# Attention of a decoder trunk: outputs half a projection tile behind scores, and pins on exponentials, masks and sums

## The chip, the cores and the metric

The kernel runs on one core of one Trainium2 chip. The metric is device time in microseconds (us) of one execution, lower is better. Five engines work side by side, each through a queue of its own: TensorE (PE in the profile: matmuls into PSUM banks, with weight loads shown apart as PEld), VectorE (DVE), ScalarE (ACT), GpSimd (POOL), and SyncE (SP), which here issues the DMAs.

## The reference

Two layers over 1024 tokens of width 1024, in float32. The first mixes tokens by retention and RWKV-7 heads; the second, which the change is about, by sliding-window attention with sinks. Each is followed by a SwiGLU feed-forward layer. What matters here:

```python
z = h @ w_qkv + b_qkv                       # 16 query heads, 4 key/value heads, head size 64
s = einsum('bnqhgd,bnkhd->bnhgqk', q, kb) * HEAD_DIM ** -0.5    # blocks of 128 queries, 256 keys
s = where(valid, s, -inf)                   # a window of 128 keys back
m = maximum(max(s), sink)
e = exp(s - m)
p = e / (sum(e) + exp(sink - m))
o = einsum('bnhgqk,bnkhd->bnqhgd', p, vb).reshape(B, T, SWA_WIDTH) @ w_o + b_o
h = h + o
h = h + (silu(n @ w_gate) * (n @ w_up)) @ w_down                # n = rms_norm(h)
```

## The kernel before

Activations lie transposed, features on the 128 partitions and tokens along the free side, in two halves of 512 tokens. A float32 product is made of three matmuls in a shorter format: each operand is split into a high part (a rounding copy on ACT) and a low part (operand minus high part, on DVE or POOL), and high x high, high x low and low x high are added up in one PSUM bank. A projection onto 128 features is 8 steps of three matmuls, 24 in all, 512 columns each; its weights are loaded by SP (L402), split in two tiles by ACT (L432) and DVE or POOL (L433), six split tiles in rotation.

The feed-forward layer is computed with a scheme of fewer products: `form0` (L1252) normalizes the first token half into eight tiles (`normed`, L1248), splits them (ACT L462, DVE L464) and stores them; `early` (L1469) makes the first of the products. A "pair" is one gate and one up projection of it, in lockstep: first halves of both (four steps each), then each bank is copied out by ACT (`u0`, L1472), because the second half adds to the same bank.

Attention (`attn`, L1692) is written as a plan of words, executed left to right. There are 16 blocks j (token half, key/value head, two windows of 128 queries):

- S: `scores`. 40 or 48 small matmuls (L1726) into banks r, c and two m; ACT copies (L1739) and DVE predicated copies (L1740) bring them to `s`; DVE takes the maximum (L1758), then the sinks' terms (L1759, L1760); ACT makes eight exponentials (L1763, "exps j" for the first) and the sink's (L1761); DVE adds the sink's to the sum (L1766, "dens j"), inverts, multiplies (L1768) and transposes 32 x 32 blocks (L1773); SP stores the result to DRAM (`pd`).
- D: `fetch`. Four DMAs bring `pd` back as `pc` with the keys on the partitions (two buffers).
- M: `sides`. A mask product `pT` on DVE (L1787) and `pc - pT` in two halves, one on DVE and one on POOL (L1792). A mask is pinned behind the sinks of block j + 2.
- O: `out`. 12 or 16 matmuls (L1805) with the values into the one bank y; the high part is copied by ACT (L1811, "his j"), the low part made by DVE (L1812, "los j").
- q, r: half a projection of queries of the first and second token half; k: half a projection of keys or values, or a transpose of values (L1678); w: one output projection `w_o` of the first half (24 matmuls, L447 to L450, then DVE L1831); f: the normalizing factor (one matmul, L479, with L480 and L481 on ACT) and `form0`; p: half of a pair.

The order on PE is written out by hand: `ATTN_ORDER` lists banks in the order in which the program first writes them, with numbers of matmuls, and `queue` (L328) chains them. On the other engines the framework's scheduler sets the order, except where `behind` (L605) pins one instruction behind another on the same engine's queue; such a pin sets the order of issue and adds no wait of its own. PSUM has three banks f, two m, one each of r, c and y.

Of the kernel before, what the change touches and what calls it, by code (L numbers as in the profile page):

```python
# [10 lines left out]
F32 = mybir.dt.float32  # L11
F32R = mybir.dt.float32r
AF = mybir.ActivationFunctionType
ALU = mybir.AluOpType
# [120 lines left out]

ATTN_PLAN = """
S0 qqq S1 qqq D0 S2 M0 D1 qqk S3 O0 M1 D2 kkk S4 O1 M2 D3 kkk S5 O2 M3 D4 krr S6 O3 M4 D5 rrr S7 O4 M5 D6 rrr
S8 O5 M6 D7 rr S9 O6 M7 D8 S10 O7 M8 D9 wwwwk S11 kwwww rr f rr S12 rr O8 M9 D10 p S13 O9 M10 D11 pp S14 O10 M11 D12 p
S15 O11 M12 D13 pp O12 M13 D14 p O13 M14 D15 p O14 M15 p O15 p
"""  # L140
ATTN_ORDER = """
# [8 lines left out]
"""  # L150


# [102 lines left out]
class Kern:  # L255
    def __init__(self, ctx, tc, A, out):
        self.ctx, self.tc, self.nc, self.A, self.out = ctx, tc, tc.nc, A, out
        nc = self.nc
        self.pp = ctx.enter_context(tc.tile_pool(name="pp", bufs=1, side="left"))
        self.dr = ctx.enter_context(tc.tile_pool(name="dr", bufs=2, space=bass.MemoryType.DRAM))  # L260
        self.n = 0
        pad = ctx.enter_context(tc.tile_pool(name="pad", bufs=1, side="right"))
        pt = pad.tile([P, 120], F32, tag="pad", name="pad")
        nc.gpsimd.memset(pt, 0.0)
        nc.scalar.activation(pt[:, :16], pt[:, :16], AF.Copy)
        self.gapt(self.pp, 32)
        self.pv = self.t(self.pp, [P, NPV], "pv")
        nc.scalar.dma_start(self.pv, A["pvec"])
        self.cst = {}
        for nm in ("ones", "eps"):  # L270
            self.cst[nm] = self.const(self.pp, nm)
        self.h, self.plan, self.seq, self.stream = [None, None], None, {}, "-"
        self.wx, self.pin, self.rest, self.at = None, None, None, {}
        self.w6, self.nw, self.owed, self.lo = False, 0, [], self.nc.gpsimd
        self.hid = [self.dram(f"hid{i}", [FT, P, HT]) for i in range(4)]
        self.hc = [self.dram(f"hc{L}", [NP, 4, P, 2, HT]) for L in range(2)]
        self.bd = self.dram("bd", [KT, P, HT])
        self.u0s = None
        self.u0d = self.dram("u0", [NP, 2, P, HT])
        self.wsp = self.dr.tile([30, 2, P, 2, HT], F32, tag="wsp", name="wsp", bufs=1)  # L280
        self.cats = [self.dram(f"cat{hf}", [KT, P, HT]) for hf in range(2)]
# [963 lines left out]
        return self.rstd(self.kt(self.h[hf]), self.t(pool, [P, HT], "rs", 1), tag)  # L1245

    def normed(self, out, hf, k, g, r):
        self.nc.vector.scalar_tensor_tensor(  # L1248
            out=out, in0=self.kt(self.h[hf])(k), scalar=self.col(g, k), in1=r, op0=ALU.mult, op1=ALU.mult
        )  # L1250

    def form0(self, g, r, n8, sp):  # L1252

        self.X = {nm: [self.hl(n8, k + o) for k in range(4)] for nm, o in (("11", 0), ("21", 4))}
        for nm, o in (("11", 0), ("21", 4)):
            for k in range(4):
                f = self.u0(sp)
                self.normed(f, 0, k + o, g, r)
                self.nc.sync.dma_start(self.bd[k + o], f)
                self.split(f, *self.X[nm][k], False)  # L1260

# [207 lines left out]
    def early(self, ps, w, u0, use):  # L1469

        self.prod(ps, w[0](), self.X["11"], True, False)
        self.nc.scalar.copy(u0, ps)  # L1472
        yield
        self.prod(ps, w[1](), self.X["21"], False, True)
        use("11", ps)
        yield
# [141 lines left out]
    def attn_open(self, ap):  # L1618
        nc = self.nc
        m = self.const(ap, "amask").rearrange("p (m o t) -> p m o t", m=2, o=1)  # L1620
        self.own = m[:, 0].rearrange("p o (x t) -> p o x t", x=2).to_broadcast([P, 2, 2, 64]).bitcast(mybir.dt.uint32)
        self.key = m[:, 1].rearrange("p o (q t) -> p q o t", q=4).to_broadcast([P, 4, 8, 32])
        self.sink = self.t(ap, [P, 16], "sink")
        nc.scalar.dma_start(self.sink, self.A["sinks"].to_broadcast([P, 16]))
        self.nsink = self.t(ap, [P, 16], "nsink")
        nc.vector.tensor_scalar(out=self.nsink, in0=self.sink, scalar1=-1.0, scalar2=None, op0=ALU.mult)
        self.b8 = self.t(ap, [P, 8], "b8")
        nc.vector.tensor_scalar(
            out=self.b8, in0=self.pv[:, PV["bqkv"] : PV["bqkv"] + 8], scalar1=0.125, scalar2=None, op0=ALU.mult
        )  # L1630
        self.pk = self.pvt = None
        self.nu0 = 0
        self.akv, self.aq, self.ch = {}, ([], []), {}

    def proj(self, nr, ti, out, **kw):
# [56 lines left out]
    def attn(self, ap, outs, fill, plan):  # L1692
# [5 lines left out]
        pairs = [(hf, g, b) for hf in range(2) for g in range(4) for b in (0, 2)]  # L1698
        n = len(pairs)
        ds, pcs, pTs, n8, sinks = {}, {}, {}, {}, {}  # L1700

        def block(hf, g, b, tags, s):

# [41 lines left out]
        def scores(j):  # L1745
            hf, g, b0 = pairs[j]
            s = self.t(ap, [P, 2, 4, P], "s", 2)
            for i in range(2):
                block(hf, g, b0 + i, ("rc", "mm")[i], s[:, i])
            s8 = s.rearrange("p b h k -> p (b h) k")  # L1750
            st = self.t(ap, [P, 3, 8], "st", 3)
            m, den, es = (st[:, i] for i in range(3))

            def heads(t):
                return t[:, 4 * g : 4 * g + 4].rearrange("p (o h) -> p o h", o=1).to_broadcast([P, 2, 4])

            m2, es2 = (t.rearrange("p (b h) -> p b h", b=2) for t in (m, es))
            V.tensor_reduce(out=m, in_=s8, axis=AX.X, op=ALU.max, negate=True)  # L1758
            V.tensor_tensor(out=m2, in0=m2, in1=heads(self.nsink), op=ALU.min)  # L1759
            sinks[j] = V.tensor_tensor(out=es2, in0=m2, in1=heads(self.sink), op=ALU.add)  # L1760
            x = S.activation(es, es, AF.Exp)  # L1761
            for h in range(8):
                y = S.activation(s8[:, h], s8[:, h], AF.Exp, bias=m[:, h : h + 1], accum_out=den[:, h : h + 1])  # L1763
                if h == 0:
                    self.behind(y, x)
            V.tensor_tensor(out=den, in0=den, in1=es, op=ALU.add)  # L1766
            V.reciprocal(out=den, in_=den)
            V.tensor_tensor(  # L1768
                out=s8, in0=s8, in1=den.rearrange("p (h o) -> p h o", o=1).to_broadcast([P, 8, P]), op=ALU.mult
            )  # L1770

            sq = self.t(ap, [P, 4, 8, 32], "sq", 1)
            V.transpose(sq.rearrange("p k h t -> p h k t"), s8.rearrange("p h (k t) -> p h k t", k=4))  # L1773
            d = ds[j] = self.dr.tile([4, 32, 4, 2 * P], F32, tag="pd", name=f"pd_{self.n}", bufs=4)
            nc.sync.dma_start(d.rearrange("q t k x -> (q t) (k x)"), sq.rearrange("p k h t -> p (k h t)"))
# [8 lines left out]
        def sides(j):  # L1784
            pc = pcs[j]
# [3 lines left out]
                self.behind(x, sinks[j + 2])  # L1789
            for i, e in enumerate((V, G)):  # L1790
                h = slice(4 * i, 4 * i + 4)
                e.tensor_tensor(out=pc[:, :, h], in0=pc[:, :, h], in1=pT[:, :, h], op=ALU.subtract)  # L1792

        def out(j):
            hf, g, b0 = pairs[j]
# [12 lines left out]
                        )  # L1808
            tk = slice(P * b0, P * b0 + 2 * P)
            hi, lo = (n8[hf][x][:, :, tk].rearrange("p i (b t) -> p b i t", b=2) for x in (g, 4 + g))  # L1810
            S.copy(hi, po)  # L1811
            V.tensor_tensor(out=lo, in0=po, in1=hi.bitcast(F32), op=ALU.subtract)  # L1812
            self.ch[hf] = [self.hl(n8[hf], k) for k in range(KT)]

        do = dict(S=scores, O=out, M=sides, D=fetch)
        for w in plan.split():
            if w[0] in do:
                do[w[0]](int(w[1:]))
            else:
                for c in w:  # L1820
                    next(fill[c], None)

    def w_o(self, hf, ch):
        nc = self.nc
# [270 lines left out]
```

## Time and profile before

| what | value |
|---|---|
| median of 3 runs | 2266.25 us (2265.46 to 2266.54) |
| the profiled execution | 2264.58 us, of which the span of its instructions is 2261.8 us |
| granted TensorE clock, mean | 0.996 |
| busy share | PE 98%, PEld 79%, DVE 74%, ACT 45%, POOL 45% |
| the chain that ended last | PE 77%, DVE 10%, ACT 4%, the rest issue, DMA, POOL and queues |
| attention stage | some 240 us, from about 1360 to 1600 us of the span |

Times in rows of the profile are us from the start of the span. A row of the timeline gives the start, the duration, the engine, the line of the kernel, the operation, output and inputs by the program's names, their shapes, and how many; in brackets stands how long the engine was idle before it and whose end released it. A matmul's row shows how long it was in the array; matmuls overlap, so that one of 512 columns is shown at 0.39 us though the next starts sooner.

### The profile page before, as it was taken

The page shows a single profiled execution, that of the slowest core. Times are in us where ns is not written, and L with a number is a line of the kernel's source. Part 1 is how long each engine was busy: PE and PEld are TensorE (multiplying, and loading weights), DVE is VectorE, ACT ScalarE, POOL GpSimd, SP SyncE. Part 2 cuts the span into 40 slices and gives each one's busy share as a digit, 9 for nine tenths or more (in the row PEclk, how much of TensorE's full clock was granted, in tenths as well). Part 3 has the DMA queues.
Part 4 walks back from the last instruction along what each step waited for, and adds up shares of the span by engine and source line. Part 5 has one row for each costly group of instructions (what it writes and reads, how often), then busy time and mean ns, then how long its engine had stood idle before and what let it go on. Part 6 is the DMA issues. An engine that isn't in the chain of part 4 may idle for free.

```text
span 2261.8 us, 36143 instructions
## 1 busy us (share of the span) xinstructions
PE 2221.5 (98%) x13296; PEld 1784.8 (79%) x13296; DVE 1683.9 (74%) x2476; ACT 1011.3 (45%) x1914; POOL 1009.9 (45%) x784
## 2 busy tenths in 40 slices
PE   8999999999999999999999999998999999999998
PEld 6777777777878888888888887776788888888886
DVE  7877965875667358888887877987457788888876
ACT  5454544424455333333433466656444333333335
POOL 3123221202341067777787610104203677777676
PEclk9999999999999999999999999999999999999999
DMA  8565654443446545665676334444546565658663
GB/s 282 188 219 203 201 158 135 141 118 117 148 181 195 205 160 209 214 210 206 242 259 246 131 113 133 162 140 155 176 150 229 176 213 211 208 202 292 225 216 117
DMA packets 181856, 423.22 MB, mean 187 GB/s; under 512 B 44464, under 2 KB 55344, under 8 KB 181680
## 3 DMA queue, kind: packets, MB, share of 16 engines
q1 hardware_dynamic: 178272, 414.37, 53.4%
q10 hardware_dynamic: 2832, 4.45, 0.5%
q8 instruction: 105, 1.72, 0.3%
q0 software_dynamic: 576, 2.10, 0.2%
q14 instruction: 71, 0.58, 0.1%
HBM read 283.87 MB, written 131.60 MB: 184 GB/s over the span
## 4 chain that ended last, share of the span: by engine, by line
PE 77%; DVE 10%; ACT 4%; issue 3%; DMA 3%; POOL 2%; SPq 1%; DVEq 0%; POOLq 0%; ACTq 0%
PE ps_f L291 11%; PE ps_m L1306 8%; PE ps_m L1309 7%; PE ps_m L1308 7%; PE ps_m L291 6%; PE ps_f L1306 5%; PE ps_f L1308 5%; PE ps_f L1309 5%; PE ps_r L1306 2%; PE ps_c L1309 2%; PE ps_c L1306 2%; PE ps_r L1309 2%; PE ps_r L1308 2%; PE ps_c L1308 2%; PE ps_f L449 2%
## 5 line engine op out<-in xcount | busy, mean ns | idle before, releaser
L291 PE MATMUL ps_f<-n,w 128*128 128x512 f32 x1440 | 358.6, 402 | 8.6 <-ACT w L432 5.7
L291 PEld LDWEIGHTS ps_f<-n,w 128*128 128x128 f32 x1440 | 266.5, 189 | 83.4 <-issue 12.6
L433 POOL TENSOR_TENSOR w<-wr,w 128x512 fp32r<-128x512 f32 x63 | 88.3, 1411 | 294.8 <-ACT w L432 293.4
L432 ACT CAST w<-wr 128x512 fp32r<-128x512 f32 x231 | 140.7, 617 | 153.8 <-PE ps_f L450 48.7
L1306 PE MATMUL ps_f<-n,w 128*128 128x512 f32 x415 | 164.6, 397 | 0.5 <-ACT q L1472 0.5
L1309 PE MATMUL ps_f<-n,w 128*128 128x512 f32 x415 | 162.5, 392 | 0.0
L433 DVE TENSOR_TENSOR w<-wr,w 128x512 fp32r<-128x512 f32 x168 | 118.2, 708 | 59.2 <-ACT w L432 58.7
L1308 PE MATMUL ps_f<-n,w 128*128 128x512 f32 x415 | 162.2, 391 | 0.0
L433 POOL TENSOR_TENSOR w<-wq,w 128x512 fp32r<-128x512 f32 x91 | 130.8, 1449 | 31.0 <-ACT w L432 31.0
L1306 PE MATMUL ps_m<-n,w 128*128 128x512 f32 x333 | 130.4, 392 | 0.0
L1308 PE MATMUL ps_m<-n,w 128*128 128x512 f32 x333 | 129.6, 389 | 0.0
L1309 PE MATMUL ps_m<-n,w 128*128 128x512 f32 x333 | 129.5, 389 | 0.0
L1316 DVE TENSOR_TENSOR nq<-ps_m,u 128x512 f32<-128x512 f32 x88 | 58.9, 684 | 93.9 <-PE ps_m L1309 93.8
L464 POOL TENSOR_TENSOR n<-nq,n 128x512 fp32r<-128x512 f32 x60 | 100.1, 1679 | 7.6 <-ACT n L462 7.6
L1501 POOL TENSOR_TENSOR w<-wd,w 128x512 fp32r<-128x512 f32 (+1 forms) x62 | 87.1, 1414 | 33.1 <-ACT w L1500 32.7
L1306 PEld LDWEIGHTS ps_f<-n,w 128*128 128x128 f32 x415 | 77.9, 188 | 21.9 <-issue 3.8
L1306 PE MATMUL ps_m<-cb,w 128*128 128x512 f32 x236 | 91.9, 389 | 0.3 <-DVE nq L1316 0.3
L1308 PE MATMUL ps_m<-cb,w 128*128 128x512 f32 x236 | 91.8, 389 | 0.0
L1309 PE MATMUL ps_m<-cb,w 128*128 128x512 f32 x236 | 91.8, 389 | 0.0
L1309 PEld LDWEIGHTS ps_f<-n,w 128*128 128x128 f32 x415 | 77.9, 188 | 17.1 <-issue 0.7
L1501 POOL TENSOR_TENSOR w<-ws,w 128x512 fp32r<-128x512 f32 (+1 forms) x48 | 71.6, 1497 | 44.4 <-ACT w L1500 40.7
L1308 PEld LDWEIGHTS ps_f<-n,w 128*128 128x128 f32 x415 | 77.9, 188 | 16.6 <-issue 1.0
(539 smaller groups left out, 6347.9 us busy)
## 6 DMA issues: line engine op xcount, KB each, us to landing
hc<-n SPq DMA_DIRECT2D x84, 512.0 KB, 3.2
wsp<-w SPq DMA_DIRECT2D x54, 512.0 KB, 3.3
w<-wsp SPq DMA_DIRECT2D x54, 512.0 KB, 3.4
n<-hc SPq DMA_DIRECT2D x54, 512.0 KB, 6.2
wq<-in_w_gate SPq DMA_DIRECT2D x44, 512.0 KB, 4.5
u<-u SPq DMA_DIRECT2D x76, 256.0 KB, 3.1
ha<-hc SPq DMA_DIRECT2D x34, 512.0 KB, 5.2
hid<-n SPq DMA_DIRECT2D x66, 256.0 KB, 2.0
```

Source lines behind the costliest of these rows:

```text
L291: i = self.nc.tensor.matmul(out, lhsT, rhs, **kw)
L432: nc.scalar.copy(hi[:, :n], raw[:, c])
L433: self.lo.tensor_tensor(out=lo[:, :n], in0=raw[:, c], in1=hi.bitcast(F32)[:, :n], op=ALU.subtract)
L449: y = nc.tensor.matmul(ps, hi, rl, start=False, stop=False)
L464: e.tensor_tensor(out=lo, in0=src, in1=hi.bitcast(F32), op=ALU.subtract)
L1306: i = mm(ps, hi, xh, start=first and k == 0, stop=False, skip_group_check=True)
L1308: mm(ps, hi, xl, start=False, stop=False, skip_group_check=True)
L1309: mm(ps, lo, xh, start=False, stop=last and k == len(w) - 1, skip_group_check=True)
L1316: self.last_add = V.tensor_tensor(out=o, in0=x, in1=y, op=ALU.add)
L1501: nc.gpsimd.tensor_tensor(out=lo, in0=v, in1=hi.bitcast(F32), op=ALU.subtract)
```

## The change

The plan and the order of PE are rewritten, and instructions are pinned behind others.

- In the plan, output O7, two of the eight `w_o` projections and one query projection of the second half move ahead of scores S10; the other `w_o` projections and the last key/value steps are spread around S10 and S11, and one query projection less stands between `form0` and S12.
- In the order of PE, an output in most blocks follows its scores with 12 matmuls of a projection between, where before it followed at once. Pair 0's second gate half comes ahead of O9.
- New pins: the first exponential of a block behind the high copy of the first output named after its scores; the sink's sum behind the DVE half of the first mask named after its scores; masks 1 to 12 behind the low part of the output before; exponentials 12, 14 and 15 behind the first, fourth and fifth copy `u0` of the pairs; the sixth `normed` tile of `form0` behind the low part of output 8.

No instruction is added or removed. The old order of PE from S8 to S12 is `65:8 66:24 (S9) 71:6 77:18 78:18 79:18 76:8 (S10) 77:6 78:6 79:6 80:12 81:4 80:12 (S11) 87:12 86:4 87:12 88:24 89:24 90:24 91:18 92:1 91:6 93:24 (S12)`, where 71 and 76 are O6 and O7, 77 to 90 (but for 81 and 86) are `w_o` and key/value steps, 91 and 93 queries, 92 the factor. The new one is `66:12 65:8 66:12 (S9) 73:18 71:6 74:18 72:8 75:24 (S10) 73:6 74:6 80:24 81:4 82:24 (S11) 87:24 88:4 89:24 90:24 91:24 92:14 93:1 92:10 (S12)`, where 71 and 72 are O6 and O7, 73, 74, 80, 82, 87 and 89 to 91 `w_o`, 81 and 88 transposes of values, 75 and 92 queries, 93 the factor.

```diff
 ATTN_PLAN = """
 ...
-S8 O5 M6 D7 rr S9 O6 M7 D8 S10 O7 M8 D9 wwwwk S11 kwwww rr f rr S12 rr O8 M9 D10 p S13 O9 M10 D11 pp S14 O10 M11 D12 p
+S8 O5 M6 D7 rr S9 O6 M7 D8 O7 wwrr S10 M8 D9 wkw S11 wkwww rr f S12 rr O8 M9 D10 p S13 O9 M10 D11 pp S14 O10 M11 D12 p
 S15 O11 M12 D13 pp O12 M13 D14 p O13 M14 D15 p O14 M15 p O15 p
@@ form0
-                self.normed(f, 0, k + o, g, r)
+                self.formed.append(self.normed(f, 0, k + o, g, r))
@@ early
-        self.nc.scalar.copy(u0, ps)
+        self.u0copies.append(self.nc.scalar.copy(u0, ps))
@@ attn: scores, sides and out note their instructions in exps, dens, subs, his and los; then, after the plan has run:
+        at = -1
+        for w in plan.split():
+            j = int(w[1:]) if w[0] in do else -1
+            if w[0] == "S":
+                at, seen = j, set()
+            elif j >= 0 and at >= 0 and w[0] not in seen:
+                seen.add(w[0])
+                if w[0] == "O":
+                    self.behind(exps[at], his[j])
+                if w[0] == "M":
+                    self.behind(dens[at], subs[j][1])
+            if w[0] == "M" and j and j < 13:
+                self.behind(subs[j][0], los[j - 1])
+        for j, i in ((12, 0), (14, 3), (15, 4)):
+            self.behind(exps[j], self.u0copies[i])
+        self.behind(self.formed[5], los[8])
```

More of the change, by code (lines that the diff above doesn't have):

```diff
@@ L278, in __init__ @@
         self.u0s = None
+        self.u0copies, self.formed = [], []
         self.u0d = self.dram("u0", [NP, 2, P, HT])
@@ L1247, in normed @@
     def normed(self, out, hf, k, g, r):
-        self.nc.vector.scalar_tensor_tensor(
+        return self.nc.vector.scalar_tensor_tensor(
             out=out, in0=self.kt(self.h[hf])(k), scalar=self.col(g, k), in1=r, op0=ALU.mult, op1=ALU.mult
@@ L1632, in attn_open @@
         self.nu0 = 0
+        self.u0copies, self.formed = [], []
         self.akv, self.aq, self.ch = {}, ([], []), {}
@@ L1700, in attn @@
         ds, pcs, pTs, n8, sinks = {}, {}, {}, {}, {}
+        exps, dens, his, los, subs = {}, {}, {}, {}, {}
         def block(hf, g, b, tags, s):
@@ L1765, in scores @@
                     self.behind(y, x)
-            V.tensor_tensor(out=den, in0=den, in1=es, op=ALU.add)
+                    exps[j] = y
+            dens[j] = V.tensor_tensor(out=den, in0=den, in1=es, op=ALU.add)
             V.reciprocal(out=den, in_=den)
@@ L1791, in sides @@
                 h = slice(4 * i, 4 * i + 4)
-                e.tensor_tensor(out=pc[:, :, h], in0=pc[:, :, h], in1=pT[:, :, h], op=ALU.subtract)
+                y = e.tensor_tensor(out=pc[:, :, h], in0=pc[:, :, h], in1=pT[:, :, h], op=ALU.subtract)
+                if not i:
+                    subs[j] = x, y
         def out(j):
@@ L1810, in out @@
             hi, lo = (n8[hf][x][:, :, tk].rearrange("p i (b t) -> p b i t", b=2) for x in (g, 4 + g))
-            S.copy(hi, po)
-            V.tensor_tensor(out=lo, in0=po, in1=hi.bitcast(F32), op=ALU.subtract)
+            his[j] = S.copy(hi, po)
+            los[j] = V.tensor_tensor(out=lo, in0=po, in1=hi.bitcast(F32), op=ALU.subtract)
             self.ch[hf] = [self.hl(n8[hf], k) for k in range(KT)]
```

14 rows, old and new, of the table ATTN_ORDER are left out of this document.

## The prediction

> **What bounds the kernel now.** I read the table of stretches first, over the attention stage and what follows. A row gives a stretch, its length, each engine's busy time with its instructions, and after POOL the granted TensorE clock. Ahead of it stands the page's line of 40 slices for PE, in tenths.
>
> ```profile
> PE   8999999999999999999999999998999999999998
> ...
> core 0: us, PE busy (x) PEld busy (x) DVE busy (x) ACT busy (x) POOL busy (x), PEclk, DMA share, GB/s
> 1400.00:1460.00 60.00, 59.35 (x481) 45.29 (x480) 56.91 (x97) 36.89 (x133) 8.17 (x7) 1.00 0.53 176
> 1460.00:1540.00 80.00, 76.64 (x519) 60.24 (x518) 68.07 (x107) 48.69 (x136) 12.41 (x9) 1.00 0.45 153
> 1540.00:1560.00 20.00, 16.78 (x115) 12.52 (x115) 14.27 (x23) 10.63 (x42) 8.45 (x5) 0.91 0.48 153
> 1560.00:1580.00 20.00, 15.39 (x108) 11.69 (x107) 12.37 (x20) 14.36 (x40) 8.24 (x6) 0.86 0.41 127
> 1580.00:1600.00 20.00, 19.45 (x138) 14.18 (x138) 12.95 (x19) 12.66 (x33) 10.79 (x7) 0.97 0.51 170
> 1640.00:1670.00 30.00, 30.00 (x133) 24.60 (x132) 12.91 (x18) 10.00 (x16) 5.17 (x4) 1.00 0.29 101
> ```
>
> PE has work nearly always, so time can only be won where it idles or is granted a slow clock. In 1640–1670 it does not idle, one 512-column matmul starts every 30.00/133 = 0.226 us, and the slices behind stay at nine: what attention wins should reach the end of the kernel. Idle is 0.65 us in 1400–1460, 3.36 in 1460–1540, and 3.22, 4.61 and 0.55 in the last three stretches before 1600. There the clock also costs (0.09 + 0.14 + 0.03) x 20 = 5.2 us. The half-rate time behind the last two means is 2 x 0.17 x 20 = 6.8 us, ending at 1580 + 1.2, so it began at 1574.4, about 1.3 us before PE resumed (below); half of that cost nothing, and 4.55 remains. Next, the waits of the instructions in question.
>
> ```profile
> 1545.66 0.19 ACT L1761 ACTIVATE st<-st 128x8 f32<-128x8 f32 x1
> 1547.68 0.56 ACT L1811 CAST n<-ps_y 128x512 fp32r<-128x512 f32 x1
> 1549.34 0.64 DVE L1812 TENSOR_TENSOR n<-ps_y,n 128x512 fp32r<-128x512 f32 x1
> 1545.24 0.37 PE L1726 MATMUL ps_c<-ks,q 64*64 64x192 f32 x1
> 1550.03 0.65 PE L1805 MATMUL ps_y<-pT,vt 128*64 128x256 f32 x4 [3.22 <-DVE n L1812]
> 1551.19 2.28 DVE L1768 TENSOR_TENSOR s<-s,st 128x1024 f32<-128x1024 f32 x1
> 1570.61 1.28 ACT L1763 ACT_TABLE_LOAD   x1 [4.16 <-DVE st L1759]
> 1575.10 0.56 ACT L1472 COPY q<-ps_f 128x512 f32<-128x512 f32 x1
> 1575.71 0.79 PE L1306 MATMUL ps_f<-n,wx 128*128 128x512 f32 x1 [4.61 <-ACT q L1472]
> 1590.90 0.50 PE L1306 MATMUL ps_f<-n,w 128*128 128x512 f32 x1 [0.55 <-ACT q L1472]
> ```
>
> O9 waits 3.22 us for the low part of O8, the reader of the one ps_y bank; that waits for O8's high copy, which ACT runs at 1547.68, behind S12's exponentials. At 1575.71 the second half of a gate-or-up projection waits 4.61 us for the copy of its first half out of the bank (L1472); ACT had been idle 4.16 us before S14's exponentials and then put the copy behind them.
>
> Last, the chain that ended last, before S9: for every block it runs through DVE and ACT, and through no PE instruction.
>
> ```profile
> 1460.66 1.23 DVE st L1758
> 1462.18 1.21 ACT s L1763 x6
> ...
> 1468.47 1.15 DVE sq L1773
> 1470.19 1.36 DVE s L1740 x4
> ```
>
> **The change part by part.** Instructions and bytes stay the same; only places move. All numbers are of the profiled execution.
>
> *Pins of exponentials.* His8 comes ahead of exps12, and the copies u0[0], u0[3], u0[4] ahead of exps12, exps14, exps15. O9's 3.22 and the 4.61 go: O8 ends at 1539.49 (below), so ACT can run the high copy 8 us sooner; and the copy at 1575.10 fits into ACT's idle 4.16. Late next: exps12 now waits until PE has finished pair 0's first gate half, 12 matmuls (2.7 us) after O8, plus 0.6 for the copy, about 1542.8. Before, they were running at 1545.66, so this costs nothing unless DVE's maximum comes 3 us sooner; behind it on ACT stand S13's evacuations, whose PE work comes 12 matmuls later still. The other "O" pins hold already (in S13, for example, ACT's high copy precedes the exponentials) and cost nothing. With the two waits their half clock goes: 3.22 + 4.61 + 4.55 = **12.4 us won**. The 0.55 I leave in: it is u0[4] or its neighbour u0[5], and only the first is pinned (bounds 0 to 0.55).
>
> *Masks behind low parts, sink's sum behind masks.*
>
> ```profile
> 1501.19 1.23 DVE L1787 TENSOR_TENSOR pT<-pc,c_amask 128x1024 f32<-128x1024 f32 x1
> 1548.08 1.23 DVE L1787 TENSOR_TENSOR pT<-pc,c_amask 128x1024 f32<-128x1024 f32 x1
> 1557.45 0.68 DVE L1812 TENSOR_TENSOR n<-ps_y,n 128x512 fp32r<-128x512 f32 x1
> 1561.82 1.22 DVE L1787 TENSOR_TENSOR pT<-pc,c_amask 128x1024 f32<-128x1024 f32 x1 [3.62 <-DMA pc<-pd]
> ```
>
> Counting from M0, these masks are M9, M10 and M11, and the low part is that of O9. M9 runs 48 us ahead of O8's low part, M10 9 ahead of O9's: from S12 on the masks run one block early, and M11 holds DVE 3.62 us for its DMA. The change moves M9 to M12 back a slot. Their data has then landed, so sum, reciprocal and product behind them no longer wait; that is DVE's gain, and PE's only through the terms above. The price: M9 (1.23 and half the subtraction on DVE, the other half on POOL) must fit between O8 and O9, and M10 to M12 likewise. I take 0; the bound is the second rival. On POOL their halves now stand among the pairs' weight splits, which can come 1.7 us later each; POOL is busy 8.45 of 20 us in 1540–1560, and that is the cover. A mask issues no DMA; SP's fetches still follow the outputs that free pc.
>
> *O half a projection later.* 12 matmuls, 2.7 us, now run between scores and output. The 0.65 of idle in 1400–1460 (O waiting for masks) goes; the chain shows, though, that DVE and ACT set the pace there, so PE only arrives sooner at the next thing DVE owes it.
>
> *O7, two w_o tiles and a projection moved ahead of S10.*
>
> ```profile
> 1464.04 1.08 PE L1805 MATMUL ps_y<-pT,vt 128*64 128x256 f32 x8 [1.14 <-DVE pT L1787]
> 1465.80 0.65 PE L1805 MATMUL ps_y<-pc,vt 128*64 128x256 f32 x4 [0.68 <-POOL pc L1792]
> 1473.71 1.23 DVE L1787 TENSOR_TENSOR pT<-pc,c_amask 128x1024 f32<-128x1024 f32 x1
> 1475.07 1.74 POOL L1792 TENSOR_TENSOR pc<-pc,pT 128x512 f32<-128x512 f32 x1 [9.32 <-DVE pT L1787]
> 1478.93 0.65 PE L1805 MATMUL ps_y<-pT,vt 128*64 128x256 f32 x4
> 1498.74 0.66 PE L1678 MATMUL ps_m<-c_ident,nq 128*128 128x128 f32 x4 [1.55 <-DVE s L1740]
> ```
>
> O6 waits 1.14 and 0.68, the transposes of v 1.55; 18 or 12 matmuls (4.1, 2.7 us) now stand ahead of each, so 0.65 + 1.14 + 0.68 + 1.55 = 4.02 us go. But 54 w_o matmuls ran between O6 and O7, and now 36 run between S9 and O7: 18 fewer, 4.07 us. PE reaches O7 at 1478.93 − 4.07 − (0.65 + 1.14 + 0.68) = 1472.4. M7 stands on DVE at 1473.71, behind S9's sinks by a pin that exists already, and POOL's half ends at 1476.81. O7's last quarter takes 0.5, so it ends at 1477.3; without a wait 1472.4 + 1.87 = 1474.3. A new wait of **3.0 us** (bounds: 0 if DVE comes 3 us sooner; 3.0 as it stands). The half clock after it: 0 after the 1.55 wait (row 1460–1540: 1.00), 0.09 x 20 = 1.8 after the 3.22, 4.55 − 1.8 = 2.75 after the 4.61. I take 1.8, the nearest row. Moved with it: that projection's load (L402 on SP) and two splits (ACT, DVE), which take the places of the third w_o tile's, so DVE has no more to do before M7; and D9's four fetches on SP, which follow O7 and hide behind its 60 later matmuls.
>
> The clock-gate page of the Trainium skill ("TensorE: Matmul & The Clock Gate", "HAM oscillation") sets the limit at idle gaps over about 3.4 us; by it this wait would cost no clock and the time would be 1.8 lower. The 3.22 us wait here was followed by a mean of 0.91, so I go by the row.
>
> *formed[5] behind O8's low part.*
>
> ```profile
> 1522.59 1.02 PE L479 MATMUL ps_f<-nq,c_ones 128*128 128x512 f32 x2
> 1532.31 1.78 DVE L464 TENSOR_TENSOR n<-q,n 128x512 fp32r<-128x512 f32 x1
> 1534.67 0.68 DVE L464 TENSOR_TENSOR n<-q,n 128x512 fp32r<-128x512 f32 x1
> 1535.88 1.40 DVE L1248 SCALAR_TENSOR_TENSOR q<-h,pv,rs 128x512 f32<-128x512 f32 x2
> 1537.62 0.65 PE L1805 MATMUL ps_y<-pT,vt 128*64 128x256 f32 x4
> 1539.49 0.50 PE L1306 MATMUL ps_f<-n,w 128*128 128x512 f32 x1
> ```
>
> The factor's matmul (1522.59) to pair 0's first half took 16.9 us; with 20 matmuls fewer between, 12.4. The fourth low part (1534.67 + 0.68) came 12.8 after the factor and is read from the tenth matmul, 2.0 later: needed at 14.4, 1.6 to spare. That is the cover; S12's copies and maximum (1.36 + 1.23) squeezed ahead would cost 1.0. Formed 5 to 7 move from 1535.88 to behind O8 (0.6 copy, 0.65 low): first needed 24 matmuls and S13 after O8, 5.4 + 1.6 (1545.24 to 1550.03 − 3.22); by rows 0.6 + 0.65 + 0.7 + 0.6 (ACT) + 0.7 = 3.3. Cost 0.
>
> **Sum.** −12.4 − 4.0 + 3.0 + 1.8 = **−11.6 us**. The profiled execution took 2264.58 us (span 2261.8, 2.8 around it), 1.67 under the median of the runs, so 2253.0 for a profile and 2266.25 − 11.6 = **2254.7** for the median.
>
> **The rivals.**
> 1. *O7 does not wait*, because DVE reaches M7 3 us sooner. For: its order is laid anew by the scheduler. Against: the chain, all DVE and ACT, with 56.91 of 60 us busy. Price: 3.0 + 1.8 less; 2249.9.
> 2. *O9 waits on a crowded DVE.* Between O8 and O9 PE has 36 matmuls (8.1) and S13 (1.6). DVE and POOL need 0.6 + 0.65 + 2.1 (three formed) + 3 x 0.68 + 1.23 + 1.74 = 8.4. With five operations at 1.78 instead of 0.68, as at 1532.31, it is 13.9: 4.2 late, and 1.8 of half clock; 2260.7. The Trainium skill ("SBUF — State Buffer", "Who interferes with whom") calls the port that DVE and GpSimd share an exclusive lock, which fits the 1.78.
> 3. *The waits only change places*: most pins hold already, and what is gained after S12 is lost at O7 and in formed; about 2266.
> 4. *Slower:* the loop low part → mask → output → copy → low part becomes the clock of the tail. It takes 0.65 + 1.23 + 1.74 + 1.87 + 0.6 = 6.1 against PE's 8.1 + 1.6 + 1.87 = 11.6; were DVE's product, transpose, copies and maximum all between (2.28 + 1.15 + 1.36 + 1.23 = 6.0) and two operations stretched by 1.1, each of O9 to O12 would wait 2.7 and pay 1.8: 4 x 4.5 = 18, 2273. It decides from three such waits (11.6/4.5). Against: that loop ran in 1400–1460 with 0.65 idle.
>
> **How the numbers follow.** Forecast 0.53, rivals 0.15, 0.14, 0.11, 0.07. The first three are faster by over 0.2% (4.5 us, about what these runs can tell from no change): 0.82, of which I move 0.02 to no change because rival 2 ends close to it: 0.80, 0.13, 0.07. The forecast's own range is 2251.5 (no half clock at O7, the 0.55 gone too) to 2258 (1.0 at the first half, 1 more of clock, 1 at O9). The range 2249 to 2263 takes in rivals 1 and 2 and leaves 0.18 out.
>
> **What would show it.** Right: no wait of PE over 1 us from S12 to O12, clock 1.00 there; L1811 of O8 ahead of exponentials of S12; M9 after O8; a wait of about 3 us at O7 naming pT or pc, and a granted clock under 1 after it. Wrong: a wait at O9 to O12 or on L464; O7 without one; or idle that turns up after 1600.

## The result, and the profile after

The changed kernel takes 2279.05 us (median of 6 runs, 2276.86 to 2279.97); the kernel before took 2266.22 beside it. The ratio is 1.0056, 95% interval 1.0043 to 1.0069: 12.8 us slower, where 2254.7 was forecast. The profiled execution took 2276.86 us, its span 2274.4, 12.6 above the span before.

Lines of the changed kernel stand a little lower: scores L1729, the exponentials L1766, the sinks' exponential L1764, mask L1791 and L1796, output L1811, its high copy L1817 and low part L1818, the pairs' copy L1473. First the page's slices for PE, then the stretches of the prediction in the same columns, then what PE and DVE waited for.

```profile
PE   8999999999999999999999999989999999999998
```

```profile
1400.00:1460.00 60.00, 55.62 (x454) 41.27 (x452) 50.31 (x83) 35.35 (x128) 7.92 (x6) 1.00 0.49 159
1460.00:1540.00 80.00, 71.78 (x438) 54.79 (x439) 58.89 (x96) 39.61 (x121) 8.49 (x6) 0.96 0.36 123
1540.00:1560.00 20.00, 18.37 (x169) 14.12 (x168) 16.87 (x25) 13.39 (x30) 5.35 (x4) 1.00 0.55 174
1560.00:1580.00 20.00, 18.05 (x126) 13.02 (x126) 14.30 (x21) 16.35 (x50) 9.56 (x7) 0.91 0.38 131
1580.00:1600.00 20.00, 16.38 (x114) 11.68 (x113) 15.51 (x25) 9.74 (x29) 9.37 (x6) 0.92 0.54 170
```

The eight among the nines has moved up to slice 27, 1478 to 1535 us. PE idles 4.38 us in 1400–1460 (0.65 before) and 8.22 in 1460–1540 (3.36 before), the latter at a clock of 0.96; the tail still has two stretches at 0.91 and 0.92. DVE, near full before (56.91 of 60), does 50.31. The four largest waits of PE from 1340 to 1660 us, and below them the one of DVE from 1390 to 1490 (total, times, longest):

```profile
PE ps_y L1811 <- DVE pc L1796: 6.9, 5, 1.5
PE ps_y L1811 <- DVE pT L1791: 5.9, 3, 4.5
PE ps_f L1307 <- ACT q L1473: 3.8, 2, 3.3
PE ps_y L1811 <- POOL pc L1796: 3.1, 2, 2.7
```

```profile
DVE n L1818 <- ACT n L1817: 14.4, 6, 3.3
```

PE waits for masks, and DVE six times, 14.4 us in all, for the high copy of an output. In the trace of before DVE has no such wait in that stretch. ACT's own rows around the high copy of O0, and then DVE's, show why:

```profile
1401.86 0.73 ACT L1646 ACTIVATE kc<-kc,pv 128x512 f32<-128x512 f32 x1 [4.04 <-DVE kc L1645]
1402.50 0.38 ACT L1766 ACTIVATE s<-s,st 128x128 f32<-128x128 f32 x1
...
1404.80 0.19 ACT L1764 ACTIVATE st<-st 128x8 f32<-128x8 f32 x1
1404.90 0.39 ACT L1766 ACTIVATE s<-s,st 128x128 f32<-128x128 f32 x1
1405.29 0.56 ACT L1817 CAST n<-ps_y 128x512 fp32r<-128x512 f32 x1
1405.75 0.40 ACT L1766 ACTIVATE s<-s,st 128x128 f32<-128x128 f32 x1
```

```profile
1405.88 0.69 DVE L1818 TENSOR_TENSOR n<-ps_y,n 128x512 fp32r<-128x512 f32 x1 [3.30 <-ACT n L1817]
1406.49 1.22 DVE L1791 TENSOR_TENSOR pT<-pc,c_amask 128x1024 f32<-128x1024 f32 x1
```

Seven of the eight exponentials run ahead of the high copy; only one follows it. That one is head 0's, the only one that the change pins behind the copy, and the scheduler put it last. DVE stands still for 3.30 us, and the mask, pinned behind the low part, is late by as much. The same holds for the high copies of O2, O4, O5 and O6; those of O1 and O3 run ahead of theirs. Before, the high copies of O0 to O6 ran ahead of all exponentials (O0's at 1398.99, the exponentials of S3 from 1403.79).

The matmuls between the first scores of S3, of S9, of S12 and the first matmul of O15 are the same in both kernels (these starts for before, then for after):

```profile
1393.24 0.37 PE L1726 MATMUL ps_c<-kc,q 64*64 64x192 f32 x1
1461.34 0.37 PE L1726 MATMUL ps_c<-ks,q 64*64 64x192 f32 x1
1530.45 0.37 PE L1726 MATMUL ps_c<-ks,q 64*64 64x192 f32 x1
1626.22 0.65 PE L1805 MATMUL ps_y<-pT,vt 128*64 128x256 f32 x4
```

```profile
1391.45 0.37 PE L1729 MATMUL ps_c<-kc,q 64*64 64x192 f32 x1
1464.66 0.37 PE L1729 MATMUL ps_c<-ks,q 64*64 64x192 f32 x1
1542.02 0.37 PE L1729 MATMUL ps_c<-ks,q 64*64 64x192 f32 x1
1638.81 0.44 PE L1811 MATMUL ps_y<-pT,vt 128*64 128x256 f32 x2
```

So the 12.6 us are −1.8 ahead of S3 (work that the change does not touch; in the fourteen profiles of this study S3 starts between 1391.45 and 1394.80), +5.1 from S3 to S9, +8.2 from S9 to S12, and +1.0 from S12 to O15. The tail (S12 to O15), from which 12.4 were to come, gave nothing. These stretches, read in the same way from each trace, sort the experiments:

| kernel | median us | before beside it | ratio (95%) | S3–S9 | S9–S12 | S12–O15 |
|---|---|---|---|---|---|---|
| before | 2266.22 | | | 68.1 | 69.1 | 95.8 |
| changed | 2279.05 | 2266.22 | 1.0056 (1.0043–1.0069) | 73.2 | 77.4 | 96.8 |
| nohalf | 2269.91 | 2264.58 | 1.0023 (1.0014–1.0031) | 68.1 | 73.8 | 96.8 |
| nolow | 2269.85 | 2264.58 | 1.0019 (1.0010–1.0028) | 67.8 | 72.1 | 98.0 |
| nopins | 2269.94 | 2264.58 | 1.0021 (1.0012–1.0030) | 68.7 | 73.2 | 94.9 |
| all9 | 2257.99 | 2264.58 | 0.9967 (0.9955–0.9980) | 67.8 | 71.3 | 87.5 |
| nolow9 | 2264.07 | 2265.65 | 0.9994 (0.9985–1.0002) | 67.8 | 72.0 | 93.6 |
| noform9 | 2256.49 | 2265.65 | 0.9959 (0.9947–0.9972) | 67.8 | 71.1 | 86.8 |
| o7late | 2258.54 | 2265.65 | 0.9971 (0.9960–0.9982) | 67.8 | 72.2 | 87.5 |
| oldmid9 | 2254.10 | 2265.65 | 0.9950 (0.9938–0.9963) | 68.1 | 69.1 | 85.5 |
| o7both | 2252.93 | 2263.90 | 0.9952 (0.9940–0.9965) | 67.8 | 67.7 | 87.4 |
| best | 2254.44 | 2263.90 | 0.9964 (0.9951–0.9976) | 67.8 | 67.6 | 88.2 |
| oldorder | 2260.69 | 2263.90 | 0.9987 (0.9978–0.9996) | 68.1 | 69.2 | 91.4 |
| tailpins | 2260.61 | 2263.90 | 0.9985 (0.9977–0.9994) | 68.1 | 69.2 | 93.0 |

### The profile page after: what moved, and what is told of

Its sections match the earlier page's. It is cut to its first block, busy times and chain, and to the rows that moved or that the text cites. A ratio compares the mean times of both kernels' runs of the same rounds, so it can differ in the third digit from the quotient of the medians.

```text
span 2274.4 us, 36133 instructions
## 1 busy us (share of the span) xinstructions
PE 2227.5 (98%) x13296; PEld 1786.4 (79%) x13296; DVE 1690.2 (74%) x2476; ACT 1010.9 (44%) x1914; POOL 1010.6 (44%) x784
## 3 DMA queue, kind: packets, MB, share of 16 engines
q8 instruction: 105, 1.72, 0.3%
## 4 chain that ended last, share of the span: by engine, by line
PE 80%; DVE 9%; DMA 4%; ACT 3%; issue 3%; SPq 1%; POOL 0%; DVEq 0%; POOLq 0%; ACTq 0%
PE ps_f L292 11%; PE ps_m L1307 8%; PE ps_m L1310 8%; PE ps_m L1309 8%; PE ps_m L292 6%; PE ps_f L1307 5%; PE ps_f L1309 5%; PE ps_f L1310 5%; PE ps_r L1307 2%; PE ps_c L1310 2%; PE ps_c L1307 2%; PE ps_r L1310 2%; PE ps_r L1309 2%; PE ps_c L1309 2%; PE ps_f L448 2%
## 5 line engine op out<-in xcount | busy, mean ns | idle before, releaser
L292 PEld LDWEIGHTS ps_f<-n,w 128*128 128x128 f32 x1440 | 268.4, 190 | 83.4 <-issue 12.6
```

Source lines behind the costliest of these rows:

```text
L292: i = self.nc.tensor.matmul(out, lhsT, rhs, **kw)
```

## The experiments

**Which part makes the loss: nohalf, nolow, nopins.** Each takes one part of the change away. nohalf puts O0 to O5 directly behind their scores again:

```diff
-... 31,32:12 28:12 33:6 34:24 ... 40:12 39:8 40:12 ... 53:12 52:8 53:12 ...
+... 31,32:12 33:6 28:12 34:24 ... 39:8 40:24       ... 52:8 53:24       ...
```

> The changed kernel with the outputs O0 to O5 put directly behind the scores of S3 to S8 again (six pairs of entries of the order swapped back); all pins, the middle (O7 ahead of S10) and the tail stay as changed. Theory 1 (the high copy's place): with the output 12 matmuls later the high copy comes behind the exponentials on ACT, the low part waits for it (3.30, 3.30, 2.84 us in the trace) and the mask behind the low part comes late; with the shift undone the high copies stand ahead of the exponentials again, so S3 to S9 takes 68 us as before (73.2 now) and O6 and O7 wait less: about 2279 - 5 to -9 = 2270 to 2274. Theory 2 (the mask pins alone close the loop): no change, 2279. Theory 3 (the 12 matmuls themselves lengthen the loop): the same as theory 1 here; the kernel with all exponentials pinned tells these two apart. Theory 4 (the loss is O7 ahead of S10): no more than 1 us.

nolow drops the pins of masks:

```diff
-            if w[0] == "M" and j and j < 13:
-                self.behind(subs[j][0], los[j - 1])
```

> The changed kernel without the pins of masks behind low parts; everything else stays. In the order that the scheduler then gives, masks stand ahead of the low part again in S3 to S9, but the high copies still stand behind seven of eight exponentials. Theory 2 (the mask pins close the loop): the masks no longer wait for the late low parts, PE's waits for pT and pc in S4 to O7 go, S3 to S10 falls from 104 to about 90 us, 2279 - 12 = 2267. Theory 1 (the high copy's place): the low part still waits and holds DVE behind it, the output's bank is free late, so the wait moves from the mask to the output's bank: 2274 to 2279.

nopins drops all the new pins and keeps the plan and the order.

> The changed kernel's plan and matmul order with none of the new pins. In the scheduler's order the high copies then stand behind all eight exponentials, the low parts behind the sink's sum and the product, and the masks ahead of the low parts. If the new order of PE alone makes the loss (theory 1 or 3): S3 to S10 is as long as in the changed kernel or longer, 2275 to 2290. If the pins make it (theory 2): S3 to S10 about 90 us, and 2262 to 2270 with the tail's waits as before.

All three come out at 2269.9, and in all three S3 to S9 is back at 68 to 69 us. The times alone would point different ways (nohalf just under theory 1's 2270 to 2274, nopins inside theory 2's 2262 to 2270, nolow between its two); the stretches decide. Each theory that named one culprit falls: theory 2, since nohalf keeps the mask pins; theories 1 and 3 alone, since nolow and nopins keep the shifted outputs and the late copy (behind seven exponentials in nolow, behind all eight in nopins); theory 4, since nohalf keeps O7's place and is over 7 us faster against the kernel before. The 5.1 us of S3 to S9 need three things at once: the output half a projection later, with which the scheduler places its copy among the exponentials; exponentials left ahead of that copy, since the pin holds one of eight (all9, next, holds them all); and a mask that may not pass the low part. S9 to S12 stays 3 to 5 us over before in all three, so O7's place is a loss beside it, and no tail is better than before's by more than 0.9.

**The copies ahead of all exponentials: all9.** The change's pins stay, but hold the sinks' exponential and all eight heads' instead of head 0's.

```diff
             x = S.activation(es, es, AF.Exp)
+            exps[j] = [x]
...
                 if h == 0:
                     self.behind(y, x)
-                    exps[j] = y
+                exps[j].append(y)
...
-                    self.behind(exps[at], his[j])
+                    for y in exps[at]:
+                        self.behind(y, his[j])
...
-            self.behind(exps[j], self.u0copies[i])
+            for y in exps[j]:
+                self.behind(y, self.u0copies[i])
```

> The changed kernel, but each of its pins on an exponential holds the exponential of the sinks and all eight of the heads, instead of the one of head 0, which in the changed kernel runs last or near it, so that seven run ahead of the copy. Theory 1 (the high copy's place): high copies run ahead of all exponentials, the low part's waits of 2.7 to 3.3 us go, S3 to S10 (104.05 us now, 87.56 before) loses 8 us or more, and the 3.3 us wait for the copy of pair 0's first half behind S12's exponentials goes with its half clock: 2279 - 8 - 5 = 2264 to 2268. Theory 3 (the 12 matmuls lengthen the loop): S3 to S10 stays over 100 us and only the tail gains, 2274. Theory 2 (mask pins): as theory 3.

2257.99: faster than before by 0.33%, and by more than expected. The high copy of the block shown above now runs at once behind the projection's activation, ahead of the nine (its lines stand one lower than in the changed kernel); the low part's wait is 0.52 us instead of 3.30, and the mask follows. This is the same place in the trace of all9, ACT and then DVE, and its stretches:

```profile
1402.77 0.73 ACT L1646 ACTIVATE kc<-kc,pv 128x512 f32<-128x512 f32 x1 [4.04 <-DVE kc L1645]
1403.41 0.57 ACT L1818 CAST n<-ps_y 128x512 fp32r<-128x512 f32 x1
1403.87 0.40 ACT L1767 ACTIVATE s<-s,st 128x128 f32<-128x128 f32 x1
```

```profile
1404.00 0.69 DVE L1819 TENSOR_TENSOR n<-ps_y,n 128x512 fp32r<-128x512 f32 x1 [0.52 <-ACT n L1818]
```

```profile
1400.00:1460.00 60.00, 60.00 (x482) 45.16 (x480) 54.95 (x94) 36.92 (x133) 9.39 (x7) 1.00 0.50 164
1460.00:1540.00 80.00, 76.60 (x508) 59.57 (x508) 61.29 (x100) 46.16 (x131) 11.42 (x8) 0.98 0.43 145
1540.00:1560.00 20.00, 18.42 (x122) 12.86 (x119) 18.33 (x31) 14.93 (x39) 9.82 (x6) 0.91 0.57 188
1560.00:1580.00 20.00, 20.00 (x183) 15.11 (x183) 17.48 (x30) 15.65 (x53) 11.00 (x8) 1.00 0.73 225
```

PE does not idle in 1400–1460, with the outputs still 12 matmuls behind: theory 3 is out, and so is theory 2, since the masks are still pinned. What is left of idle is two places, one at O7 and one at pair 0's second half.

**The rest, one place at a time: o7late, o7both, noform9.** o7late moves 24 matmuls ahead of O7, o7both another 24 ahead of the open w_o tiles' last quarters, noform9 drops the pin of formed[5]; each starts from all9.

```diff
-74:18 72:8 75:24 76,77:12 78,79:12 73:6 74:6 80:24 81:4     # all9
+74:18 75:24 72:8 76,77:12 78,79:12 73:6 74:6 80:24 81:4     # o7late
+74:18 75:24 72:8 76,77:12 78,79:12 80:24 73:6 74:6 81:4     # o7both
...
-        self.behind(self.formed[5], los[8])                 # noform9
```

> The kernel with all nine exponentials pinned, and besides it one projection (24 matmuls, 5.4 us) moved from behind O7 to ahead of it. In the kernel with all nine pinned O7 still waits 3.4 us for mask 7 on DVE, and O7 and the matmuls behind it run 1.9 us longer at half clock. Theory 1 (that wait is a plain shortage of matmuls ahead of O7, as the prediction has it): both go, 2258.0 - 5.3 = 2252.7. Rival (the wait only moves: what hangs on O7's copy, the last quarters of the two open w_o tiles and mask 8, is late by the same time): 2256 to 2258.

> The kernel with all nine exponentials pinned, with one projection (24 matmuls, 5.4 us) ahead of O7 as in the run before, and another projection of 24 matmuls moved ahead of the last quarters of the two open w_o tiles, which need O7's low part and waited 3.5 us for O7's copy there. Theory (two plain shortages of matmuls, one behind mask 7 and one behind O7): both waits and both half clocks go; S9 to S12, 71.3 us with all nine pinned and 72.2 with the first move alone, falls to 66, and the time to 2258.0 - 5.3 = 2252.7. Rival (the chain through DVE and ACT is late by itself, and the wait moves on once more, to the transposes of v or to S11): 2256 to 2258.

> The kernel with all nine exponentials pinned, without the pin of formed[5] behind O8's low part. S13 to S14 takes 15.8 us there and S14 to S15 12.1, with the same matmuls: 3.8 us go to waits for the split factors of pair 0's second half and to a half clock behind them. Theory (the pin makes them late): 2258.0 - 3.8 = 2254.2. Rival (DVE has too much to do between S12 and S13 in either order, so the wait moves to O8's low part, O9 or S12's maximum): 2257 to 2259.

The first row is the wait at O7 in all9, the second the one that took its place in o7late, behind O7's own high copy.

```profile
1475.54 0.65 PE L1812 MATMUL ps_y<-pT,vt 128*64 128x256 f32 x4 [3.40 <-DVE pT L1792]
```

```profile
1485.74 0.80 PE L448 MATMUL ps_f<-n,w 128*128 128x512 f32 x1 [3.50 <-ACT n L1818]
```

In o7late the rival held: S9 to S12 took 72.2 us, not 66. With matmuls on both sides (o7both) it takes 67.7, 1.4 less than before. That the kernel's 2252.9 us is the time expected is in part luck: 3.6 us came in this stretch, not 5.3, the spans of the two profiles differ by 3.7 (2254.6 and 2250.9), and the kernel before, too, ran 0.7 us faster beside o7both than beside all9. noform9 got 2.9 us between S13 and S14 (12.9 for 15.8) but gave back most of it in waits of its own, 0.97 and 1.30 us further on, so that S12 to O15 is only 0.7 shorter and its ratio cannot be told from that of all9; neither expectation was quite right. Its new waits (total, times, longest):

```profile
PE ps_f L1307 <- ACT q L1473: 1.8, 2, 1.0
PE ps_y L1812 <- DVE n L1819: 1.3, 1, 1.3
```

**What the mask pins are worth: nolow9.** all9 without the pins of masks behind low parts (the two lines of nolow).

> The kernel with all nine exponentials pinned, without the pins of masks behind low parts. With the high copies in time, theory 1 says these pins cost nothing and bring little: 2256 to 2260, S3 to S9 again 67.9 us. Theory 2 (the pins of masks are themselves the brake): S9 to S12, 71.3 us there, falls to 69 and O7's wait goes, 2254 or less. A third case: the pins are what keeps the masks from running one block early in the tail, and without them S12 to O15 (87.5 us) grows by the 3 us of a mask that waits for its DMA: 2261.

The third case, at twice its price: 2264.1, S12 to O15 93.6 us, 6 more than all9. S3 to S9 stays at 67.8: with the copies in time these pins cost nothing there. In this trace DVE waits 20.0 us for fetched blocks between 1530 and 1620, with masks one block early, 11.1 in all9 (total, times, longest; nolow9, then all9):

```profile
DVE pT L1792 <- DMA pc<-pd: 20.0, 4, 8.2
```

```profile
DVE pT L1792 <- DMA pc<-pd: 11.1, 3, 7.3
```

**Which order needs the pins: oldorder, oldmid9, tailpins, best.** oldorder puts the plan and order of the kernel before under the pins as written. oldmid9 takes that plan and order up to S12 and directly behind S13, and in the tail O10 and O11 half a projection later, with all nine pinned. tailpins is oldmid9 with the pins on exponentials 12 to 15 alone. best is o7both with O9 directly behind S13.

```diff
+... 66:24 67,68:12 69,70:12 71:6 77:18 78:18 79:18 76:8 ...     # oldorder, oldmid9, tailpins: O6, three w_o, O7
-... 104,105:12 100:12 106:8 101:12 ...
+... 104,105:12 106:8 100:12 101:12 ...                          # oldmid9, tailpins, best: O9 behind S13
...
+        for j in (12, 13, 14, 15):                              # tailpins, in place of the other pins
+            for y in exps[j]:
+                self.behind(y, his[j - 4])
```

> The changed kernel's pins as written, each on the exponential of head 0 alone, with the plan and order of the kernel before. Theory 1 (pins on one exponential of eight do not bring the copy ahead): S3 to S12 as before (137.2 us), and in the tail the high copies and the copies of the pairs' first halves still stand behind seven exponentials, so S12 to O15 stays at 93 to 97 us: 2262 to 2267. Rival (one pinned exponential is enough where the outputs stand directly behind the scores): S12 to O15 at 86, 2255.

> The kernel with all nine exponentials pinned, with the plan and order of the kernel before up to S12 (outputs directly behind scores, O7 behind S9 and three open w_o tiles), and the changed order of the tail. S9 to S12 took 69.1 us before and 71.3 with all nine pinned, S3 to S9 68.1 and 67.9. Theory (the moved O7 is a loss of its own, the outputs half a projection later change nothing): 2258.0 - 2.0 = 2256. Rival (the 12 matmuls between scores and output are needed): more than 2258.

> The fastest kernel so far (old plan and order up to S12, the changed order in the tail, all nine exponentials pinned) with the pins on exponentials of S12 to S15 alone: behind the high copies of O8 to O11 and behind the copies of pairs 0, 3 and 4; no pin on masks, sums or formed factors, none ahead of S12. Theory (the gain is the copies on ACT): 2254, S12 to O15 about 85.5 us. Rival (the masks must also be held behind the low parts in the tail, as the 93.6 us of the kernel without those pins says): 2261.

> As the kernel with both moves around O7, and O9 directly behind S13 again, with pair 0's second half behind it. With O9 half a projection later, pair 0's second half waits for the split factors (S12 to O15 87.5 us against 85.5 where O9 stands directly behind S13). Theory (these two gains lie in different stretches and add): 2252.7 - 1.9 = 2250.8. Rival (O9 waits 1.9 us for the low part of O8 and the half clock comes back): 2253.

oldorder, 2260.7, lies between its two expectations: single pins bring the tail to 91.4 us. oldmid9 is at 2254.1, better than expected: S9 to S12 gave its 2.2 us, and the tail, at 85.5, another 2.0, which the expectation did not have; it left out that O9 stands directly behind S13 here. tailpins, 2260.6, met its rival: with the pins on masks, sums and factors gone the tail takes 93.0, and nolow9 shows that the masks alone make most of that. The chain there: DVE waits for a fetched block ahead of a mask, behind the mask stand the product, the copies and the maximum of the next block, ACT waits for the sinks behind them, and the copy of a pair's first half stands behind ACT's exponentials. A row of DVE and one of ACT in tailpins, and PE's wait for the copy:

```profile
1574.84 1.23 DVE L1792 TENSOR_TENSOR pT<-pc,c_amask 128x1024 f32<-128x1024 f32 x1 [7.12 <-DMA pc<-pd]
```

```profile
1583.79 0.21 ACT L1764 ACTIVATE st<-st 128x8 f32<-128x8 f32 x1 [5.61 <-DVE st L1763]
```

```profile
PE ps_f L1307 <- ACT q L1473: 6.0, 1, 6.0
```

best missed, and its rival held: O9 waited 2.45 us, for a mask that DVE runs behind O8's low part, with half clock behind it, so the 1.9 of the tail did not add. O8's low part comes 16.2 us after S12's first scores there and 13.9 in oldmid9; that this is because `form0` stands closer to S12 in the new plan is argued, not shown. Of the versions here o7both (0.9952) and oldmid9 (0.9950) are the fastest; their intervals overlap.

## Why the prediction was wrong, point by point

- **The step that failed** is the reading of a pin: "the copies u0[0], u0[3], u0[4] ahead of exps12, exps14, exps15", and with it "The other "O" pins hold already". A pin holds one exponential of its block, head 0's, and I read it as holding all eight. The two waits named did go: the high copy of O8 (1555.26) ran ahead of all of S12's exponentials, the copy u0[3] (1578.71) ahead of S14's (from 1586.40), and neither O9 nor the place of the 4.61 waits. Others came in their stead. ACT's rows around pair 0 in the changed kernel, and the wait on PE:

```profile
1558.37 0.40 ACT L1766 ACTIVATE s<-s,st 128x128 f32<-128x128 f32 x1 [0.50 <-DVE st L1762]
...
1560.69 0.39 ACT L1766 ACTIVATE s<-s,st 128x128 f32<-128x128 f32 x1
1561.08 0.56 ACT L1473 COPY q<-ps_f 128x512 f32<-128x512 f32 x1
```

```profile
1561.69 0.50 PE L1307 MATMUL ps_f<-n,wx 128*128 128x512 f32 x1 [3.32 <-ACT q L1473]
```

  Seven exponentials of S12, 2.7 us, stand ahead of the copy u0[0], and PE waits 3.32 us for it. In the same way the high copies of O9, O10 and O11 stand behind seven exponentials of S13, S14 and S15. DVE waits for them (12.5 us in three waits), and the masks behind the low parts come late. The low part of O10, and then O11, which waits first 0.91 us for `pT` and then 2.71 for the POOL half of its mask:

```profile
1589.81 0.69 DVE L1818 TENSOR_TENSOR n<-ps_y,n 128x512 fp32r<-128x512 f32 x1 [3.30 <-ACT n L1817]
```

```profile
1596.20 0.65 PE L1811 MATMUL ps_y<-pc,vt 128*64 128x256 f32 x4 [2.71 <-POOL pc L1796]
```

  That POOL half stood behind a weight split (1592.66 to 1593.93); the prediction had priced only the splits coming later, not this. O12 waits 1.29 us and pair 2's second copy costs 0.50. With the half clock behind u0[0]'s wait and behind O11's (0.43 x 4 us = 1.7 each) this makes 3.32 + 0.91 + 2.71 + 1.29 + 0.50 + 3.4 = 12.1 us, about the 12.4 that were to be won. With all nine held, the tail gave 8.3 us (all9) and 10.3 (oldmid9) of the 12.4.
- **"The other "O" pins hold already", and cost nothing,** failed in the same way ahead of the tail: they held because the outputs stood directly behind the scores, as nohalf shows. Moved 12 matmuls later, five of the seven copies of O0 to O6 fell behind seven exponentials, and with **masks behind low parts, "I take 0"**, that closed the loop: +5.1 us from S3 to S9, where −0.65 was forecast. That the order of ready times in the scheduler's model put the copy there is argued, not shown; that it ran there is in the rows.
- **Outputs half a projection later, by itself:** right in sign. The idle in 1400–1460 went from 0.65 to 0 in all9, and S3 to S9 is 0.3 us shorter than before.
- **O7:** 3.0 of wait and 1.8 of half clock were forecast. all9 has 3.40, and the clock of 0.98 over 80 us is 1.6. In the changed kernel the low part of O6, too, waited for its copy (1.59 us, to 1481.63), mask 7 followed at 1482.24, and O7 waited 4.47 us, then 1.53 for the second half of the mask, with a half clock of some 7 us behind it (0.46 x 7.5 = 3.4 us); S9 to S12 lost 8.2 us where the terms below make 1.4:

```profile
1483.60 0.65 PE L1811 MATMUL ps_y<-pT,vt 128*64 128x256 f32 x4 [4.47 <-DVE pT L1791]
```

```profile
1484.00:1491.50 7.50, 5.97 (x23) 3.65 (x21) 5.16 (x7) 0.58 (x1) 1.18 (x1) 0.54 0.59 210
```

- **Idle that the moved matmuls remove:** right in sign. The waits at O6 and at the transposes of v are not among those of all9; S9 to S12 comes out 2.2 us longer than before there, where the terms 3.0 + 1.8 − 1.14 − 0.68 − 1.55 make 1.4. The remaining 0.8 is not traced to a single place.
- **formed[5], "Cost 0":** wrong. In all9 S13 to S14 takes 15.8 us and S14 to S15 12.1, with the same matmuls: pair 0's second half waited 0.89 and 0.67 us for splits of the factors, with a half clock behind (rows below). Without the pin (noform9) S13 to S14 is 2.9 us shorter, but only 0.7 of it is left at O15.
- **The mask pins as "DVE's gain, and PE's only through the terms above":** right for DVE, whose waits for fetched blocks from 1530 to 1620 fell from 22.1 us to 0.2 in the changed kernel; too small for PE, where the pins are worth 6 us of the tail once the copies are in time (nolow9 against all9).
- **The rivals:** the fourth had the mechanism, low part to mask to output to copy to low part, but set it in O9 to O12 only, with DVE's own work as the brake, and gave it 0.07. I argued against it with the 0.65 of idle in 1400–1460, a stretch in which the copy ran ahead of the exponentials. That condition was what the change moved. O9 and O10 did not wait in the changed kernel; O11 and O12 did.

## What to carry to other kernels

A pin holds one instruction, not the group that it belongs to: look at which members of the group the scheduler runs ahead of it, and pin them all. Before an engine's stretch without idle is taken as evidence, ask which place in another queue it rests on and whether the change moves that place. Matmuls moved ahead of a wait must also leave enough work behind the instruction that waited, or the wait only passes to the next reader.

## What the hardware showed beyond what was expected

Behind some waits PE is granted half of its clock for a few us; in the trace of before it was 0.50 from 1551 to 1553. This half clock follows waits shorter than the 3.22 us of before. In nolow9 a single wait of 2.80 us was enough, in best one of 2.45 with another of 0.54 behind it, and in all9 two of 0.89 and 0.67 behind each other. Yet 1.14 and 0.68 behind each other at O6 before cost no clock (1.00 from 1460 to 1467), and neither did 1.72 in tailpins, 1.53 in oldmid9 (1.00 in the 7.3 us from it on) or 1.95 in oldorder (1.00 from 1573 to 1578). The waits, and the stretch from each on, of nolow9, all9 and tailpins:

```profile
1478.48 0.65 PE L1812 MATMUL ps_y<-pT,vt 128*64 128x256 f32 x4 [2.80 <-DVE n L1819]
```

```profile
1478.40:1483.00 4.60, 4.52 (x20) 2.68 (x21) 3.77 (x7) 1.85 (x6) 0.55 (x1) 0.63 0.28 80
```

```profile
1549.74 0.50 PE L1307 MATMUL ps_f<-n,wx 128*128 128x512 f32 x1 [0.89 <-ACT n L463]
1550.91 0.50 PE L1309 MATMUL ps_f<-n,wx 128*128 128x512 f32 x1 [0.67 <-DVE n L465]
```

```profile
1549.00:1556.00 7.00, 5.59 (x23) 3.39 (x25) 5.44 (x10) 6.91 (x26) 4.88 (x3) 0.76 0.43 162
```

```profile
1558.97 0.50 PE L1307 MATMUL ps_f<-n,w 128*128 128x512 f32 x1 [1.72 <-ACT sg L1363]
```

```profile
1558.90:1563.00 4.10, 4.03 (x22) 2.94 (x24) 4.07 (x7) 4.10 (x11) 3.83 (x2) 1.00 0.33 128
```

What besides its length decides whether a wait costs clock stays open here. The Trainium skill ("TensorE: Matmul & The Clock Gate", "HAM oscillation") puts the limit at idle gaps over about 3.4 us; the rows of nolow9 and all9 do not agree with it, and these measurements decide.
